# Inverting the diagonal blocks of two groups of heads with the same instructions, in one long kernel

## The chip, the cores and the metric

The kernel runs on one core of a Trainium2 chip. Its metric is the device time of one execution in microseconds (us), the median of several. Engines are named as in the profile: PE (matrix products; PEld its weight loads), DVE (vector), ACT (activations), POOL (general), and SP, whose queue issues most DMAs.

## The reference

The program computes several transformer layers on 256 context and 256 latent tokens, with a width of 1024: an RWKV-7/Mamba mixer, a feed-forward, neighbourhood attention, a mixture of experts, and two further blocks. What is changed lies in the first mixer, in RWKV's recurrence, which runs over eight heads of 64 and in both directions:

```python
def _rwkv7_scan(s0, r, w, k, v, a, b):
    def step(S, inp):
        r_t, w_t, k_t, v_t, a_t, b_t = inp
        sa = jnp.einsum('bhvk,bhk->bhv', S, a_t)
        S = S * w_t[:, :, None, :] + sa[..., None] * b_t[:, :, None, :] + v_t[..., None] * k_t[:, :, None, :]
        return S, jnp.einsum('bhvk,bhk->bhv', S, r_t)
    ...
    s_fin, ys = lax.scan(step, s0, xs)
```

Beside it the program computes adaLN's shifts and scales, products of a small conditioning vector with large weights (`w_ada`, `ada_w_2`), which have nothing to do with the recurrence but are needed after it.

## The kernel before, in words

The scan is done by chunks of 64 tokens. Inside a chunk the tokens act on each other through a triangular matrix, which is inverted: a 64x64 matrix is split in two diagonal blocks of 32x32, each is inverted by forward substitution, and the corner is made with small matmuls.

The work is cut into eight groups k = (th, sh, u): th is context or latent tokens, sh the half of the chunks, u the half of the heads. Each group has 32 diagonal blocks. Its stages are:

- **P(k)**: decays, keys and scores (matmuls `lw`, `ic`, `ci`, `sc`; DVE masks the scores into EA in line 966 and into S in line 968), then `rw_blocks`. That writes the diagonal blocks from EA to DRAM (`dsc`) and reads them back as E, one block to four partitions, with each of the four read all of `dsc`; it also makes a zero matrix X with ones on the diagonal (POOL) and the transposed corner (`et`). At its end `rw_update` makes the `bt` transposes.
- **I(k)**: 31 steps of forward substitution on DVE, a product (line 1012) and a sum (line 1013) each. A partition handles 8 of a block's 32 columns, so step i works on i//4+1 columns.
- **Q(k)**: the inverse X goes through DRAM (`dx`, line 1018) back into EA (line 1022), on SP's and ACT's DMA queues; three sets of 16 small matmuls `m` and copies (lines 1036, 1038 and 1045) make the corner.
- **C(k)**: two chain steps (`rw_step`). A step makes Z from UV with EA and from the state YM with AR, copies it to zs (line 1072), makes the second half of Z from zs with EA, copies it to UV (line 1081), makes the new Z from UV with S and YM with AR, and adds (line 1095, into YM).
- **F**: normalises and gates the output.

ORDER names the order in which the stages are written out. A scheduler then sets each engine's queue. It is a fixed list: an engine that waits for one instruction starts none behind it. Matmuls of adaLN (line 377, called `ada`, with the row's transposes `adat` in line 386) get the lowest priority there and so stand where the model of the scheduler has PE free. Their weights come as tiles `raw` of 512 KB through SP's queue (line 353) into five buffers.

Of the kernel before, what the change touches and what calls it, by code (L numbers as in the profile page):

```python
# [8 lines left out]
F32 = mybir.dt.float32  # L9
# [3 lines left out]
ALU = mybir.AluOpType  # L13
# [4 lines left out]
D = 1024  # L18
# [29 lines left out]


F1, F2, F3, F4, F5, F6, F7 = 2, 2, 2, 2, 2, 2, 1  # L50
ORDER = 'P0 I0 P1 I1 Q0 C0 P2 I2 Q1 C1 P3 I3 Q2 C2 F0 P4 I4 Q3 C3 F1 P5 I5 Q4 C4 P6 I6 Q5 C5 P7 I7 Q6 C6 F2 Q7 C7 F3'
HOT = 0
WB = 1, 1
HOTM = 100000
# [1 line left out]
NROW = 5  # L56
NU, ND, NM, NYM, NB, NR, NW, NMB = 8, 3, 4, 6, 2, 6, 4, 7
NFIRST = 3000
XENG = '0'
QE = 's'  # L60
NADA = 12

# [3 lines left out]
class Builder:  # L66
# [474 lines left out]
    def mixer_consts(s):  # L541
        nc, I, mx = s.nc, s.I, s.mx
        s.lora = mx.tile([128, 3, 512], F32, name="lora")
        nc.scalar.dma_start(s.lora, I["lora"])
        c = s.cmix = mx.tile([128, 896], F32, name="cmix")
        nc.scalar.dma_start(c, I["c_mix"])
        s.tri = c[:, 0:256].rearrange("p (d t) -> p d t", d=2)
        s.maskr = c[:, 256:768].rearrange("p (d h e t) -> p d h e t", d=2, h=2, e=2)
        s.bd = c[:, 768:896]
        s.c0 = mx.tile([128, 14], F32, name="c0")  # L550
        nc.vector.tensor_tensor(s.c0, s.pcols("mu0"), s.pcols("mu1"), op=ALU.add)
        nc.vector.tensor_scalar(s.c0, s.c0, -1.0, 1.0, op0=ALU.mult, op1=ALU.add)

        s.kah = mx.tile([128, 4], F32, name="kah")
        nc.vector.tensor_scalar(s.kah, s.pcols("ka"), 0.5, None, op0=ALU.mult)
        s.ka1 = mx.tile([128, 4], F32, name="ka1")
        nc.vector.tensor_scalar(s.ka1, s.kah, -1.0, 1.0, op0=ALU.mult, op1=ALU.add)
        s.kkh = mx.tile([128, 4], F32, name="kkh")
        nc.vector.tensor_scalar(s.kkh, s.pcols("kk"), -1.0, None, op0=ALU.mult)

        s.PT = mx.tile([128, 4, 2, 2, 2, 2, 2], F32, name="PT")
        s.la = mx.tile([128, 4, 2, 8], F32, name="la")
        nc.vector.memset(s.PT, 0.0)
        s.par = mx.tile([128, 4], F32, name="par")
        nc.scalar.dma_start(s.par, I["c_x0"])
        s.misc = [mx.tile([128, 512], F32, name="misc%d" % i) for i in range(3)]
        s.iv = [mx.tile([128, 136], F32, name="iv%d" % i) for i in range(2)]
        s.zs = [mx.tile([128, 256], F32, name="zs%d" % i) for i in range(2)]
# [187 lines left out]
    def rw_blocks(s, th, sh, u):  # L756


        a, v = s.nc.scalar, s.nc.vector
        E = s.E[th, sh, u] = s.unit(nm="E").rearrange("p (s t) -> p s t", s=32)  # L760
        EA = s.EA[th, sh, u].rearrange("p d j c h t -> p (d j c) h t")
        D = s.dr.tile([4, 8, 32, 32], F32, name=s.n("dsc"))
        for i in (0, 2, 1, 3):
            r = slice(32 * i, 32 * i + 32)
            s.dq(i < 2).dma_start(D[i].rearrange("q s t -> s q t"), EA[r, :, 1 - i // 2, 32 * (i % 2):32 * (i % 2) + 32])
        D = D.rearrange("i q s t -> (i q) s t")
        for r in range(4):
            s.dq(r % 2).dma_start(E[r::4], D)
        X = s.row(nm="X")
        s.xt[th, sh, u] = X  # L770
        s.nc.gpsimd.memset(X[:, 0:256], 0.0)
        for r in range(4):
            s.nc.gpsimd.tensor_copy(X[:, r:256:36], s.par[:, r:r + 1].to_broadcast([128, 8]))
        xt = X[:, 256:512].rearrange("p (q t) -> p q t", q=8)
        p = s.ps("et")[:, 0:256].rearrange("p (q t) -> p q t", q=8)
        for q in range(8):
            for h in range(2):
                o = 64 - 64 * h
                s.mm(p[o + 32:o + 64, q], lhsT=EA[o:o + 32, q, h, 32:64], rhs=s.ident[o:o + 32, o:o + 32], start=True, stop=True, tile_position=(o, o + 32))
        for h in range(2):  # L780
            o = 96 - 64 * h
            (v.tensor_copy if h else a.copy)(xt[o:o + 32], p[o:o + 32])
# [14 lines left out]

    def rwkv(s):
        x = [(k // 4, k // 2 % 2, k % 2) for k in range(8)]
        X = {}  # L800

        def P(k):
            s.rw_tiles(*x[k])
            yield from s.rw_prep(*x[k])
            s.rw_blocks(*x[k])
            yield
            s.rw_update(*x[k])
            yield

        def I(k):  # L810
            X[k] = s.rw_inverse(*x[k])
            for i in range(31):
                next(X[k])
                if i % 8 == 7:
                    yield

        def Q(k):
            yield from X.pop(k)

        def C(k):  # L820
            if k % 4 < 2:
                s.rw_values(x[k][0], x[k][2])
            yield from s.rw_chain(*x[k])

        def F(k):
            yield from s.rw_finish(k // 2, k % 2)
        for o in ORDER.split():
            s.dump("@%s" % o)
            yield from {"P": P, "I": I, "Q": Q, "C": C, "F": F}[o[0]](int(o[1]))
# [153 lines left out]
    def rw_values(s, th, u):  # L983
# [12 lines left out]
        for h in range(2):  # L996
            s.nc.scalar.copy(UV[HS[h], :, :, h].rearrange("p j c t -> p (j c) t"), q8(p[HS[h]]))

    def rw_inverse(s, th, sh, u):

        nc = s.nc
        v, a = nc.vector, nc.scalar
        mm = s.mm
        E = s.E.pop((th, sh, u))

        Xt = s.xt.pop((th, sh, u))
        X = Xt[:, 0:256].rearrange("p (m t) -> p m t", m=8)
        e = nc.gpsimd if XENG[(4 * th + 2 * sh + u) % len(XENG)] == "1" else nc.vector
        for i in range(31):
            m, n = i // 4 + 1, 31 - i  # L1010
            t = s.iv[i % 2][:, :m * n].rearrange("p (m n) -> p m n", m=m)
            e.tensor_tensor(t, X[:, 0:m, i:i + 1].to_broadcast([128, m, n]), E[:, i:i + 1, i + 1:].to_broadcast([128, m, n]), op=ALU.mult)
            e.tensor_tensor(X[:, 0:m, i + 1:], X[:, 0:m, i + 1:], t, op=ALU.add)
            yield
        Dx = s.dr.tile([32, 32, 32], F32, name=s.n("dx"))
        dst = Dx.rearrange("q (m r) t -> r q m t", r=4)
        for r in range(4):
            s.dq(r % 2).dma_start(dst[r], X[r::4])
        EA = s.EA[th, sh, u].rearrange("p d j c h t -> p (d j c) h t")
        for i in (0, 2, 1, 3):  # L1020
            r = slice(32 * i, 32 * i + 32)
            s.dq(i < 2).dma_start(EA[r, :, 1 - i // 2, 32 * (i % 2):32 * (i % 2) + 32], Dx[8 * i:8 * i + 8].rearrange("q s t -> s q t"))
        xt = Xt[:, 256:512].rearrange("p (q t) -> p q t", q=8)

        R = [(slice(64 - 64 * h, 96 - 64 * h), slice(96 - 64 * h, 128 - 64 * h), 64 - 64 * h) for h in range(2)]
        p1, p2 = [s.ps("m1")[:, 0:256].rearrange("p (q t) -> p q t", q=8) for _ in range(2)]
        for q in range(8):
            for h in range(2):
                r1, r2, o = R[h]
                mm(p1[r1, q], lhsT=EA[r1, q, h, 0:32], rhs=s.ident[r1, r1], start=True, stop=True, tile_position=(o, o))  # L1030
        for q in range(8):
            for h in range(2):
                r1, r2, o = R[h]
                mm(p2[r1, q], lhsT=xt[r2, q], rhs=EA[r2, q, h, 32:64], start=True, stop=True, tile_position=(o + 32, o))
        for h in range(2):
            (v.tensor_copy if h else a.copy)(xt[R[h][0]], p1[R[h][0]])
        for h in range(2):
            (v.tensor_copy if h else a.copy)(EA[R[h][0], :, h, 32:64], p2[R[h][0]])
        yield
        for q in range(8):  # L1040
            for h in range(2):
                r1, r2, o = R[h]
                mm(p1[r1, q], lhsT=xt[r1, q], rhs=EA[r1, q, h, 32:64], start=True, stop=True, tile_position=(o, o))
        for h in range(2):
            (v.tensor_copy if h else a.copy)(EA[R[h][0], :, h, 32:64], p1[R[h][0]])
        yield

    def rw_step(s, th, sh, u, i, new):
# [1198 lines left out]
def host_arrays(inp):  # L2247

    A = {k: np.asarray(v) for k, v in inp.items()}
    f = np.float32  # L2250
    out = {}
# [46 lines left out]
    q = 63 - np.arange(128) % 64  # L2298
# [3 lines left out]
    i = np.arange(128)  # L2302
# [5 lines left out]
    j = np.arange(128) % 64  # L2308
# [12 lines left out]
    c = 2 * np.pi * ((i[:, None] * i[None, :]) % 128) / 128  # L2321
    n = 2 * np.pi * ((tt[:, None] * tt[None, :]) % 256) / 256
# [3 lines left out]
    i = np.arange(128)  # L2326
    k, t = i[:, None], i[None, :]
# [4 lines left out]
    for h in range(2):  # L2332
# [2 lines left out]
    seg = [k > t, k <= t, k < t, k >= t]  # L2335
    out["c_mix"] = np.concatenate([np.where(m, f(-0.5 * E05), f(0)) for m in tri] + [m.astype(f) for m in mask]
                                  + [same.astype(f)], axis=1).astype(f)
    out["c_x0"] = np.tile(np.eye(4, dtype=f), (32, 1))
    out["c_seg"] = np.concatenate([m.astype(f) for m in seg], axis=1)
    return out  # L2340

# [13 lines left out]
```

## Time and profile before

| | us |
|---|---|
| median of three executions | 2830.1 (2818.82 to 2833.47) |
| the profiled execution | 2819.89, span 2818.1 |
| PE busy in the span | 2632.0 (93%) |
| PEld | 2093.3 (74%) |
| DVE | 1885.5 (67%) |
| ACT | 1289.0 (46%) |
| POOL | 170.9 (6%) |

A share is of the whole span, over stages with different limits. The recurrence is the stretch from about 255 to 668 us, so the rows below are of that stretch. The granted clock is PE's, as a share of 2.4 GHz.

### The profile page before, as it was taken

The page shows a single profiled execution, that of the slowest core. Times are in us where ns is not written, and L with a number is a line of the kernel's source. Part 1 is how long each engine was busy: PE and PEld are TensorE (multiplying, and loading weights), DVE is VectorE, ACT ScalarE, POOL GpSimd, SP SyncE. Part 2 cuts the span into 40 slices and gives each one's busy share as a digit, 9 for nine tenths or more (in the row PEclk, how much of TensorE's full clock was granted, in tenths as well). Part 3 has the DMA queues.
Part 4 walks back from the last instruction along what each step waited for, and adds up shares of the span by engine and source line. Part 5 has one row for each costly group of instructions (what it writes and reads, how often), then busy time and mean ns, then how long its engine had stood idle before and what let it go on. Part 6 is the DMA issues. An engine that isn't in the chain of part 4 may idle for free. (4 is left out here: it accounts for less than half of the span.)

```text
span 2818.1 us, 40635 instructions
## 1 busy us (share of the span) xinstructions
PE 2632.0 (93%) x15434; PEld 2093.3 (74%) x15434; DVE 1885.5 (67%) x3039; ACT 1289.0 (46%) x1760; POOL 170.9 (6%) x276
## 2 busy tenths in 40 slices
PE   6999899997999998999999999999998987997798
PEld 3876456654888887887788888888876866996797
DVE  4657877744434457445798988998896566555655
ACT  3532122112332223444688777777775443443343
POOL 0112223210000000000000000000000000000000
PEclk8999888988999998999899999999998998998899
DMA  6324876668323233433599999999997324663562
GB/s 237 89 73 162 271 243 199 217 229 296 101 90 103 92 90 90 105 90 109 188 373 347 347 343 345 363 359 345 357 342 252 122 90 149 186 189 100 160 184 75
DMA packets 324444, 570.83 MB, mean 203 GB/s; under 512 B 61752, under 2 KB 167608, under 8 KB 324240
## 3 DMA queue, kind: packets, MB, share of 16 engines
q1 hardware_dynamic: 304064, 544.61, 57.2%
q10 hardware_dynamic: 16784, 11.74, 1.4%
q0 software_dynamic: 3392, 11.80, 1.3%
q8 instruction: 123, 2.02, 0.3%
q14 instruction: 81, 0.66, 0.1%
HBM read 563.79 MB, written 4.28 MB: 202 GB/s over the span
## 5 line engine op out<-in xcount | busy, mean ns | idle before, releaser
L204 DVE TENSOR_TENSOR wl<-raw,wh 128x1024 fp32r<-128x1024 f32 x828 | 984.6, 1221 | 427.6 <-ACT wh L203 414.0
L203 ACT CAST wh<-raw 128x1024 fp32r<-128x1024 f32 x828 | 839.0, 1051 | 511.4 <-issue 191.4
L249 PE MATMUL ws<-xL,wh 128*128 128x256 f32 (+1 forms) x1392 | 456.5, 328 | 3.6 <-DVE xL L204 3.6
L248 PE MATMUL ws<-xH,wh 128*128 128x256 f32 (+1 forms) x1392 | 458.5, 332 | 0.9 <-DVE xTf L482 0.7
L250 PE MATMUL ws<-xH,wl 128*128 128x256 f32 (+1 forms) x1392 | 457.6, 329 | 0.5 <-DVE wl L204 0.5
L248 PEld LDWEIGHTS ws<-xH,wh 128*128 128x128 f32 x1392 | 265.8, 192 | 35.7 <-issue 10.1
L249 PE MATMUL mw<-wl,eH 128*128 128x512 f32 (+1 forms) x768 | 289.7, 377 | 1.4 <-DVE wl L204 1.2
L250 PEld LDWEIGHTS ws<-xH,wl 128*128 128x128 f32 x1392 | 265.8, 191 | 30.7 <-issue 6.8
L248 PE MATMUL mw<-wh,eH 128*128 128x512 f32 (+1 forms) x768 | 286.2, 375 | 1.8 <-ACT wh L203 1.8
L249 PEld LDWEIGHTS ws<-xL,wh 128*128 128x128 f32 x1392 | 265.8, 191 | 29.2 <-DVE xL L204 4.6
L250 PE MATMUL mw<-wh,eL 128*128 128x512 f32 (+1 forms) x768 | 286.4, 373 | 0.0
L377 PE MATMUL ada<-raw,act 128*32 128x512 f32 x768 | 175.6, 728 | 32.2 <-DMA raw<-in_w_ada 13.1
L249 PEld LDWEIGHTS mw<-wl,eH 128*128 128x128 f32 x768 | 145.1, 189 | 33.3 <-DVE wl L204 8.8
L248 PEld LDWEIGHTS mw<-wh,eH 128*128 128x128 f32 x768 | 145.0, 189 | 28.3 <-ACT wh L203 3.1
L250 PEld LDWEIGHTS mw<-wh,eL 128*128 128x128 f32 x768 | 145.0, 189 | 24.1
L249 PE MATMUL y<-wl,uH 128*128 128x512 f32 x352 | 139.6, 397 | 2.0 <-DVE wl L204 2.0
L250 PE MATMUL y<-wh,uL 128*128 128x512 f32 x352 | 135.7, 391 | 0.0
L248 PE MATMUL y<-wh,uH 128*128 128x512 f32 x352 | 115.0, 390 | 0.0
L471 PE MATMUL xT<-ident,xn 128*128 128x128 f32 x160 | 34.9, 394 | 82.1 <-DVE xn L449 51.5
L377 PEld LDWEIGHTS ada<-raw,act 128*32 128x32 f32 x768 | 28.4, 122 | 105.5 <-issue 36.1
L248 PE MATMUL o<-wh,mH 128*128 128x512 f32 x256 | 100.0, 390 | 0.0
L249 PE MATMUL o<-wl,mH 128*128 128x512 f32 x256 | 99.9, 390 | 0.0
(483 smaller groups left out, 4070.2 us busy)
## 6 DMA issues: line engine op xcount, KB each, us to landing
raw<-in_moe_w SPq DMA_DIRECT2D x528, 512.0 KB
raw<-in_mlp_w SPq DMA_DIRECT2D x128, 512.0 KB
raw<-in_w_ada SPq DMA_DIRECT2D x96, 512.0 KB
raw<-in_ada_w SPq DMA_DIRECT2D x96, 512.0 KB
raw<-in_ffn_w SPq DMA_DIRECT2D x66, 512.0 KB
raw<-in_mix_w_in SPq DMA_DIRECT2D x24, 512.0 KB
raw<-in_na_w_qkv SPq DMA_DIRECT2D x24, 512.0 KB
raw<-in_w_in SPq DMA_DIRECT2D x24, 512.0 KB
```

The source lines that it names most:

```text
L203: s.nc.scalar.copy(H, raw)
L204: s.nc.vector.tensor_tensor(L, raw, H, op=ALU.subtract)
L248: mm(out, lhsT=lH, rhs=rH, start=start, stop=False)
L249: mm(out, lhsT=lH, rhs=rL, start=False, stop=False)
L250: mm(out, lhsT=lL, rhs=rH, start=False, stop=stop)
L377: nc.tensor.matmul(ps[32 * j:32 * j + 32, :], lhsT=act[:, k, :], rhs=x[j // 2][:, j % 2 * 512:j % 2 * 512 + 512], start=(k == 0), stop=(k ...
L471: nc.tensor.transpose(p[:, j, t * 128:t * 128 + 128], xn[t][:, k * 128:k * 128 + 128], s.ident)
```

## The change

E and X become a matter of a pair of groups (the same th and sh, both u). A block now has two partitions for four, a partition 16 of its columns; the two groups of a pair fill the 128 partitions together. `rw_solve` runs the 31 steps once for the pair, on i//2+1 columns in step i, and at its end puts the DMAs of X to `dx` and back into EA for both groups. `rw_inverse` is left with the small matmuls. The zeros and ones of X are made at the start of `rw_solve`. `XENG`, a choice of engine that was always DVE, goes. ORDER is written by pairs.

```diff
@@ -48,7 +48,8 @@
 F1, F2, F3, F4, F5, F6, F7 = 2, 2, 2, 2, 2, 2, 1
-ORDER = 'P0 I0 P1 I1 Q0 C0 P2 I2 Q1 C1 P3 I3 Q2 C2 F0 P4 I4 Q3 C3 F1 P5 I5 Q4 C4 P6 I6 Q5 C5 P7 I7 Q6 C6 F2 Q7 C7 F3'
+
+ORDER = 'P0 P1 I0 P2 Q0 Q1 C0 P3 C1 I2 P4 Q2 Q3 C2 P5 C3 F0 F1 I4 P6 Q4 Q5 C4 P7 C5 I6 Q6 Q7 C6 C7 F2 F3'
 HOT = 0
 WB = 1, 1
 HOTM = 100000
@@ -56,7 +57,6 @@
 NROW = 5
 NU, ND, NM, NYM, NB, NR, NW, NMB = 8, 3, 4, 6, 2, 6, 4, 7
 NFIRST = 3000
-XENG = '0'
 QE = 's'
 NADA = 12
@@ -561,7 +561,7 @@
         s.PT = mx.tile([128, 4, 2, 2, 2, 2, 2], F32, name="PT")
         s.la = mx.tile([128, 4, 2, 8], F32, name="la")
         nc.vector.memset(s.PT, 0.0)
-        s.par = mx.tile([128, 4], F32, name="par")
+        s.par = mx.tile([128, 2], F32, name="par")
         nc.scalar.dma_start(s.par, I["c_x0"])
         s.misc = [mx.tile([128, 512], F32, name="misc%d" % i) for i in range(3)]
         s.iv = [mx.tile([128, 136], F32, name="iv%d" % i) for i in range(2)]
@@ -757,21 +757,19 @@
         a, v = s.nc.scalar, s.nc.vector
-        E = s.E[th, sh, u] = s.unit(nm="E").rearrange("p (s t) -> p s t", s=32)
+        if u == 0:
+            s.E[th, sh] = s.unit(nm="E").rearrange("p (s t) -> p s t", s=32)
+            s.xt[th, sh] = s.row(nm="X")
+        E = s.E[th, sh]
         EA = s.EA[th, sh, u].rearrange("p d j c h t -> p (d j c) h t")
         D = s.dr.tile([4, 8, 32, 32], F32, name=s.n("dsc"))
         for i in (0, 2, 1, 3):
             r = slice(32 * i, 32 * i + 32)
             s.dq(i < 2).dma_start(D[i].rearrange("q s t -> s q t"), EA[r, :, 1 - i // 2, 32 * (i % 2):32 * (i % 2) + 32])
         D = D.rearrange("i q s t -> (i q) s t")
-        for r in range(4):
-            s.dq(r % 2).dma_start(E[r::4], D)
-        X = s.row(nm="X")
-        s.xt[th, sh, u] = X
-        s.nc.gpsimd.memset(X[:, 0:256], 0.0)
-        for r in range(4):
-            s.nc.gpsimd.tensor_copy(X[:, r:256:36], s.par[:, r:r + 1].to_broadcast([128, 8]))
-        xt = X[:, 256:512].rearrange("p (q t) -> p q t", q=8)
+        for r in range(2):
+            s.dq(r).dma_start(E[2 * u + r::4], D)
+        xt = s.xt[th, sh][:, 256 * u:256 * u + 256].rearrange("p (q t) -> p q t", q=8)
         p = s.ps("et")[:, 0:256].rearrange("p (q t) -> p q t", q=8)
         for q in range(8):
             for h in range(2):
@@ -797,7 +795,6 @@
     def rwkv(s):
         x = [(k // 4, k // 2 % 2, k % 2) for k in range(8)]
-        X = {}
         def P(k):
             s.rw_tiles(*x[k])
@@ -808,14 +805,10 @@
             yield
         def I(k):
-            X[k] = s.rw_inverse(*x[k])
-            for i in range(31):
-                next(X[k])
-                if i % 8 == 7:
-                    yield
+            yield from s.rw_solve(*x[k][:2])
         def Q(k):
-            yield from X.pop(k)
+            yield from s.rw_inverse(*x[k])
         def C(k):
             if k % 4 < 2:
@@ -996,31 +989,42 @@
         for h in range(2):
             s.nc.scalar.copy(UV[HS[h], :, :, h].rearrange("p j c t -> p (j c) t"), q8(p[HS[h]]))
+    def rw_solve(s, th, sh):
+
+        nc = s.nc
+        v = nc.vector
+        E = s.E.pop((th, sh))
+
+        Xr = s.row(nm="X")
+        nc.gpsimd.memset(Xr, 0.0)
+        for r in range(2):
+            nc.gpsimd.tensor_copy(Xr[:, r:512:34], s.par[:, r:r + 1].to_broadcast([128, 16]))
+        X = Xr.rearrange("p (m t) -> p m t", m=16)
+        for i in range(31):
+            m, n = i // 2 + 1, 31 - i
+            t = s.iv[i % 2][:, :m * n].rearrange("p (m n) -> p m n", m=m)
+            v.tensor_tensor(t, X[:, 0:m, i:i + 1].to_broadcast([128, m, n]), E[:, i:i + 1, i + 1:].to_broadcast([128, m, n]), op=ALU.mult)
+            v.tensor_tensor(X[:, 0:m, i + 1:], X[:, 0:m, i + 1:], t, op=ALU.add)
+            if i % 8 == 7:
+                yield
+        for u in range(2):
+            Dx = s.dr.tile([32, 32, 32], F32, name=s.n("dx"))
+            dst = Dx.rearrange("q (m r) t -> r q m t", r=2)
+            for r in range(2):
+                s.dq(r).dma_start(dst[r], X[2 * u + r::4])
+            EA = s.EA[th, sh, u].rearrange("p d j c h t -> p (d j c) h t")
+            for i in (0, 2, 1, 3):
+                r = slice(32 * i, 32 * i + 32)
+                s.dq(i < 2).dma_start(EA[r, :, 1 - i // 2, 32 * (i % 2):32 * (i % 2) + 32], Dx[8 * i:8 * i + 8].rearrange("q s t -> s q t"))
+        yield
+
     def rw_inverse(s, th, sh, u):
         nc = s.nc
         v, a = nc.vector, nc.scalar
         mm = s.mm
-        E = s.E.pop((th, sh, u))
-
-        Xt = s.xt.pop((th, sh, u))
-        X = Xt[:, 0:256].rearrange("p (m t) -> p m t", m=8)
-        e = nc.gpsimd if XENG[(4 * th + 2 * sh + u) % len(XENG)] == "1" else nc.vector
-        for i in range(31):
-            m, n = i // 4 + 1, 31 - i
-            t = s.iv[i % 2][:, :m * n].rearrange("p (m n) -> p m n", m=m)
-            e.tensor_tensor(t, X[:, 0:m, i:i + 1].to_broadcast([128, m, n]), E[:, i:i + 1, i + 1:].to_broadcast([128, m, n]), op=ALU.mult)
-            e.tensor_tensor(X[:, 0:m, i + 1:], X[:, 0:m, i + 1:], t, op=ALU.add)
-            yield
-        Dx = s.dr.tile([32, 32, 32], F32, name=s.n("dx"))
-        dst = Dx.rearrange("q (m r) t -> r q m t", r=4)
-        for r in range(4):
-            s.dq(r % 2).dma_start(dst[r], X[r::4])
         EA = s.EA[th, sh, u].rearrange("p d j c h t -> p (d j c) h t")
-        for i in (0, 2, 1, 3):
-            r = slice(32 * i, 32 * i + 32)
-            s.dq(i < 2).dma_start(EA[r, :, 1 - i // 2, 32 * (i % 2):32 * (i % 2) + 32], Dx[8 * i:8 * i + 8].rearrange("q s t -> s q t"))
-        xt = Xt[:, 256:512].rearrange("p (q t) -> p q t", q=8)
+        xt = s.xt[th, sh][:, 256 * u:256 * u + 256].rearrange("p (q t) -> p q t", q=8)
         R = [(slice(64 - 64 * h, 96 - 64 * h), slice(96 - 64 * h, 128 - 64 * h), 64 - 64 * h) for h in range(2)]
         p1, p2 = [s.ps("m1")[:, 0:256].rearrange("p (q t) -> p q t", q=8) for _ in range(2)]
@@ -1043,6 +1047,8 @@
                 mm(p1[r1, q], lhsT=xt[r1, q], rhs=EA[r1, q, h, 32:64], start=True, stop=True, tile_position=(o, o))
         for h in range(2):
             (v.tensor_copy if h else a.copy)(EA[R[h][0], :, h, 32:64], p1[R[h][0]])
+        if u:
+            del s.xt[th, sh]
         yield
     def rw_step(s, th, sh, u, i, new):
@@ -2335,7 +2341,7 @@
     seg = [k > t, k <= t, k < t, k >= t]
     out["c_mix"] = np.concatenate([np.where(m, f(-0.5 * E05), f(0)) for m in tri] + [m.astype(f) for m in mask]
                                   + [same.astype(f)], axis=1).astype(f)
-    out["c_x0"] = np.tile(np.eye(4, dtype=f), (32, 1))
+    out["c_x0"] = np.tile(np.eye(2, dtype=f), (64, 1))
     out["c_seg"] = np.concatenate([m.astype(f) for m in seg], axis=1)
     return out
```

The first place is on PE, where the first `m` of the second pair stands (EA_3322 before and EA_3093 now are the same group, context tokens, second half of the chunks, first half of the heads). Before:

```order
1006 L377 MATMUL ada_2221<-raw_2248,act_87 32x512 x2
1007 L377 MATMUL ada_2221<-raw_2249,act_87 32x512 x2
1008 L377 MATMUL ada_2221<-raw_2256,act_87 32x512 x2
1009 L274 MATMUL m_3896<-ident,EA_3322 32x32 x16
1010 L274 MATMUL m_3897<-EA_3322,X_3420 32x32 x16
1011 L377 MATMUL ada_2221<-raw_2257,act_87 32x512 x2
1012 L377 MATMUL ada_2221<-raw_2264,act_87 32x512 x2
1013 L377 MATMUL ada_2221<-raw_2265,act_87 32x512 x2
1014 L274 MATMUL sc_4155<-AR_4130,bk_4137 128x128 x4
```

And now:

```order
974 L274 MATMUL Z_3985<-YM_3388,AR_3122 64x64 x2
975 L274 MATMUL Z_3985<-UV_3334,EA_3093 64x64 x2
976 L274 MATMUL lw_3750<-lora,misc_302 128x256
977 L274 MATMUL Z_3620<-zs_307,EA_2892 64x64 x8
978 L274 MATMUL lw_3750<-lora,misc_303 128x256
979 L377 MATMUL ada_2221<-raw_2230,act_87 32x512
980 L274 MATMUL m_3872<-ident,EA_3093 32x32 x2
981 L274 MATMUL ic_3751<-misc_302,lora 128x128 x2
982 L274 MATMUL ic_3751<-misc_303,lora 128x128 x2
983 L274 MATMUL m_3872<-ident,EA_3093 32x32 x4
984 L274 MATMUL Z_3649<-UV_3565,S_2944 128x64
985 L274 MATMUL Z_3649<-YM_3586,AR_2921 64x64
```

Before, three ada tiles stand directly ahead of the group's `m`; now matmuls of the chain and of the group after next do, with one half of an ada tile.

The second place is on PE again, at the last inversion: EA_5267 was the last group of all, and EA_4483 and EA_4844 are now the last two. Before:

```order
1387 L274 MATMUL Z_5581<-UV_3218,EA_4884 64x64 x2
1388 L274 MATMUL Z_5581<-YM_5530,AR_4913 64x64 x2
1389 L274 MATMUL Z_5581<-UV_3218,EA_4884 64x64 x2
1390 L386 MATMUL adat_2608<-ident,adar_2538 128x128 x4
1391 L274 MATMUL m_5688<-ident,EA_5267 32x32 x12
1392 L274 MATMUL Z_5581<-zs_306,EA_4884 64x64 x8
1393 L274 MATMUL m_5688<-ident,EA_5267 32x32 x4
1394 L274 MATMUL m_5689<-EA_5267,X_5365 32x32 x16
1395 L377 MATMUL ada_2619<-raw_2591,act_90 32x512 x2
1396 L377 MATMUL ada_2619<-raw_2592,act_90 32x512 x2
```

And now:

```order
1378 L377 MATMUL ada_2540<-raw_2558,act_90 32x512 x2
1379 L377 MATMUL ada_2540<-raw_2567,act_90 32x512 x2
1380 L377 MATMUL ada_2540<-raw_2568,act_90 32x512 x2
1381 L377 MATMUL ada_2540<-raw_2575,act_90 32x512 x2
1382 L377 MATMUL ada_2540<-raw_2576,act_90 32x512 x2
1383 L377 MATMUL ada_2540<-raw_2583,act_90 32x512 x2
1384 L377 MATMUL ada_2540<-raw_2584,act_90 32x512 x2
1385 L386 MATMUL adat_2608<-ident,adar_2538 128x128 x4
1386 L274 MATMUL m_5171<-ident,EA_4483 32x32 x16
1387 L274 MATMUL m_5172<-EA_4483,X_4572 32x32 x16
1388 L377 MATMUL ada_2619<-raw_2591,act_90 32x512 x2
1389 L377 MATMUL ada_2619<-raw_2592,act_90 32x512 x2
```

The `m` of the last inversion stood behind Z matmuls with the row transposes `adat`; now that of the pair stands behind seven ada tiles of these rows and `adat`, and the other group's `m` and Z follow after it.

The third place is on DVE, where the last solve ends. Before:

```order
1051 L1012 TENSOR_TENSOR iv_305<-X_5365,E_5355 128x16
1052 L1013 TENSOR_TENSOR X_5365<-X_5365,iv_305 128x8x2
1053 L1012 TENSOR_TENSOR iv_304<-X_5365,E_5355 128x8
1054 L1013 TENSOR_TENSOR X_5365<-X_5365,iv_304 128x8
1055 L1095 TENSOR_TENSOR YM_5530<-Z_5560,YM_5530 128x512
1056 L380 TENSOR_TENSOR adar_2538<-ada_2540,adar_2538 128x512
1057 L1072 COPY zs_306<-Z_5581 128x256
1058 L391 COPY mcol_98<-adat_2608 128x4x2 x4
1059 L1081 COPY UV_3218<-Z_5581 64x2x2x64
1060 L1036 COPY X_5365<-m_5688 32x256
1061 L1038 COPY EA_5267<-m_5689 32x8x32
```

And now:

```order
796 L1006 TENSOR_TENSOR iv_305<-X_5091,E_4571 128x30
797 L1007 TENSOR_TENSOR X_5091<-X_5091,iv_305 128x15x2
798 L1006 TENSOR_TENSOR iv_304<-X_5091,E_4571 128x16
799 L1007 TENSOR_TENSOR X_5091<-X_5091,iv_304 128x16
800 L380 TENSOR_TENSOR adar_2538<-ada_2540,adar_2538 128x512
801 L391 COPY mcol_98<-adat_2608 128x4x2 x4
802 L1040 COPY X_4572<-m_5171 32x256
803 L1042 COPY EA_4483<-m_5172 32x8x32
804 L1049 COPY EA_4483<-m_5171 32x8x32
805 L1040 COPY X_4572<-m_5227 32x256
806 L1042 COPY EA_4844<-m_5228 32x8x32
```

The last steps have twice as many columns (16 for 8) in as many instructions, and the copies of two groups follow for those of one. DVE has 496 instructions of the solve before and 248 now.

## Rows read from the trace of the kernel before

**Rows 1.** Busy time by stretch: length, engines, clock, DMA share, GB/s; stage and its end.

```profile
255.00:668.00 413.00, 383.61 (x3693) 219.21 (x3693) 280.43 (x913) 77.57 (x161) 94.65 (x162) 0.87 0.71 234
...
600.00:668.00 68.00, 59.36 (x450) 26.76 (x445) 23.66 (x56) 8.89 (x16) 6.32 (x9) 0.80 0.69 232
```

**Rows 2.** What PE waited for, 255 to 668: total us, times, longest.

```profile
PE ada L377 <- DMA raw<-in_ada_w: 10.4, 17, 3.0
PE ada L377 <- DMA raw<-in_w_ada: 7.6, 8, 2.0
PE adat L386 <- DVE adar L380: 2.9, 3, 1.2
...
PE sc L274 <- DVE iv L1012: 1.4, 2, 0.9
PE et L274 <- DVE EA L966: 1.2, 1, 1.2
PE Z L274 <- DVE EA L1045: 1.2, 1, 1.2
PE m L274 <- DMA EA<-dx: 0.9, 1, 0.9
PE sc L274 <- DVE bk L913: 0.6, 1, 0.6
```

**Rows 3.** PE groups, 255 to 668: busy us, mean ns, idle before, releasers.

```profile
L377 PE MATMUL ada<-raw,act 128*32 128x512 f32 x671 | 151.1, 727 | 19.9 <-DMA raw<-in_ada_w 10.4 <-DMA raw<-in_w_ada 7.6 <-issue 1.5
L274 PE MATMUL Z<-UV,S 128*128 128x64 f32 x256 | 55.4, 308 | 0.0
L274 PE MATMUL Z<-YM,AR 64*64 64x64 f32 x448 | 54.9, 248 | 0.0
...
L274 PE MATMUL Z<-UV,EA 64*64 64x64 f32 x256 | 17.4, 232 | 0.0
L274 PE MATMUL Z<-zs,EA 64*64 64x64 f32 x256 | 14.0, 238 | 1.2 <-DVE EA L1045 1.2
...
L278 PE MATMUL bt<-ident,bk 128*128 128x128 f32 x64 | 11.7, 319 | 0.7 <-POOL bk L976 0.5 <-DVE X L782 0.2
```

**Rows 4.** DVE groups, 255 to 640, columns as above.

```profile
L1013 DVE TENSOR_TENSOR X<-X,iv 128x60 f32<-128x60 f32 (+24 forms) x248 | 63.6, 256 | 5.9
L1012 DVE TENSOR_TENSOR iv<-X,E 128x60 f32<-128x60 f32 (+24 forms) x248 | 60.0, 242 | 16.7 <-DMA E<-dsc 10.9
...
L1095 DVE TENSOR_TENSOR YM<-Z,YM 128x512 f32<-128x512 f32 x14 | 9.7, 690 | 37.9 <-PE Z L274 37.9
```

**Rows 5.** DVE, shapes apart, in the last solve.

```profile
L1012 DVE TENSOR_TENSOR iv<-X,E 128x60 f32<-128x60 f32 x3 | 0.7, 222 | 0.1
```

**Rows 6.** Timeline of the last inversion: start us, us, instruction, idle before.

```profile
562.30 0.42 DVE L966 TENSOR_TENSOR EA<-sc,cmix 128x256 f32<-128x256 f32 x1 [3.90 <-PE sc L274]
...
571.93 0.19 DVE L1012 TENSOR_TENSOR iv<-X,E 128x31 f32<-128x31 f32 x1 [4.03 <-DMA E<-dsc]
...
589.60 0.17 DVE L1013 TENSOR_TENSOR X<-X,iv 128x8 f32<-128x8 f32 x1
...
599.13 0.57 PE L274 MATMUL m<-ident,EA 32*32 32x32 f32 x24 [0.95 <-DMA EA<-dx]
```

**Rows 7.** Stretch at a lower clock, and two PE rows of the timeline about its start.

```profile
508.00:517.50 9.50, 9.50 (x94) 7.23 (x97) 6.73 (x20) 1.17 (x3) 4.36 (x4) 0.50 0.14 34
...
506.80 0.43 PE L274 MATMUL Z<-UV,S 128*128 128x64 f32 x2
...
508.22 0.69 PE L274 MATMUL Z<-UV,S 128*128 128x64 f32 x2
```

**Rows 8.** Timeline of PE: the row with which the stage ends.

```profile
667.80 0.66 PE L386 MATMUL adat<-ident,adar 128*128 128x128 f32 x4 [0.85 <-DVE adar L380]
```

## The prediction

> **What bounds the kernel now.** I read the table by stretch first, then what TensorE waited for, then the groups of PE and DVE, then single instructions. The change touches only the recurrence, which fills 255 to 668 us of the span [rows 1]. There PE is busy 383.61 of 413 us, DVE 280.43, ACT and POOL under 100 each; the granted clock averages 0.87 and the DMA engines are 0.71 busy [rows 1]. PE's queue is a fixed order of the recurrence's small matmuls with the adaLN matmuls (L377) put between them. All that PE waits for in these 413 us is in one list [rows 2]: 18.0 us for adaLN's own weights (10.4 and 7.6), 2.9 for the adaLN row sum on DVE, and for what the change touches 1.4 (scores behind a solve's instruction), 1.2 and 1.2 (two EA results late on DVE), 0.9 (m behind EA<-dx) and 0.6 (bk): 5.3 us together. The other way round, DVE's chain sum YM waits 37.9 us for PE [rows 4]. So the stage is a full PE queue, and the solve is almost wholly beside it.
>
> **What the change removes.** The solve is 248 products and 248 sums on DVE, 60.0 and 63.6 us, 123.6 together [rows 4]. An undisturbed one takes 222 ns with 60 elements and 166 with 8 [rows 5], so 1.08 ns an element on a fixed 157. One solve works on 1560 elements in 31 steps in each of the two operations (the sum over i of (i//4+1)(31-i)): 62 x 0.157 + 2 x 1560 x 0.00108 = 13.1 us, and eight are 105 us. That 123.6 is more is other work at the same time. The pair's solve has the same 62 instructions with (i//2+1)(31-i), 2856 elements: 9.7 + 6.2 = 15.9 us, and four are 64 us. So 41 us of DVE's busy time go, or 48 if the surplus shrinks in proportion (123.6 x 64/105 = 75). What of it lies on the path is at most what PE waited for behind it, the 5.3 us above; of these the m wait and the masks behind scores will have successors. I take 4 off.
>
> **What it moves, and the waits that this makes.** No matmul goes or comes: m, et, Z and the scores are the same, so PE's work is the same to within the order. The order changes. Both groups of a pair now need the scores of the second before the solve may begin, and all their m matmuls wait for one solve. From the last score's mask to m there is one chain, read at the last group of before: the mask starts at 562.30, the first product at 571.93 (so 9.6 us through dsc and E), the last sum ends at 589.77, m starts at 599.13 (9.4 us through dx and EA) [rows 6]. The pair's solve is 15.9 us, some 1.9 of gaps (62 x 0.03: the last group's 62 instructions took 17.8 us, with other DVE work among them), and about 3 us of the chain's own copies and sums that stand between, 21 in all. The chain is then 9.6 + 21 + 9.4 = 40 us.
>
> What stands in PE's queue in that time decides. For the second pair, between the last score of group 3 and the first m of group 2, the new order has 24 Z<-UV,S, 32 Z<-YM,AR, 24 Z<-UV,EA, 24 Z<-zs,EA, 15 ada and 8 bt matmuls, each two rows in the trace. At the means of [rows 3], busy time by count, this is 48 x 0.216 + 64 x 0.123 + 48 x 0.068 + 48 x 0.055 + 30 x 0.225 + 16 x 0.183 = 10.4 + 7.9 + 3.3 + 2.6 + 6.8 + 2.9 = 33.9 us, and some 4 for the adat, et, m and lw among them: 38 at the stage's mean clock. At full clock it would be about a tenth less (the clock term below), 34. So PE stands still for 2 to 6 us at the first m of that pair; I take 4. In before the same m comes behind three ada tiles, and the one wait for EA<-dx in the stage is the 0.9 us of the last group [rows 2, 6]. For the first pair PE has the in_w_ada matmuls in plenty, and m comes at about the time of before: 0. For the last pair the new order puts nine ada tiles, each 1.05 us as four rows at full clock, ahead of m, where before had Z matmuls; that covers most of it. For pairs 3 and 4 together I take 3. Both ends: nothing (cover holds everywhere), and 27 us if three pairs each lose 9, the length of the EA path that has no cover of its own.
>
> **Edits at no cost.** E is loaded with two DMAs a group for four: half of 8 x 512 KB, 2 MB of the roughly 97 MB that 234 GB/s [rows 1] makes of 413 us. The queue's tail runs by weights (the last ada's row sum ends the stage at 667.80 [rows 8]) and five weight buffers let no load run further ahead, so bytes saved at 300 us are not had at 660: between -9 (2.1 MB at 234 GB/s) and 0, taken 0. The two dx stores of a pair and the EA loads behind them sit in SP's queue among weight loads; a weight load stuck behind the dx wait costs PE what the five buffers don't hold. The trace shows no such loss of its own beside the 18.0 us; bounds 0 and +4, taken 0. X is cleared by POOL just ahead of the solve, not with the scores; it has the E transfer (most of 9.6 us) to lie under: 0, and 2 us a pair, 8 in all, if it starts only after E is in. The m copies stay as they were.
>
> **The clock.** In 508.00 to 517.50 PE was busy without a gap at a granted 0.50, so 1.2 GHz, and a pair of Z<-UV,S rows took 0.69 us after 0.43 just before at 2.4 GHz [rows 7]; the fall came amid a full run of Z matmuls. A mean of 0.87 over 413 us says that about 2 x 0.13 x 413 = 107 us went at 1.2 GHz; at 0.43/0.69 of the time they would be 67, so the half clock costs 40 us. The last stretch, with many ada matmuls, had 0.80 [rows 1], so more ada does not by itself bring the clock. The new order crowds small matmuls in some places and ada in others. Nothing in the rows says to which side that falls: 20 us of these 40 either way, taken 0.
>
> The Trainium skill, "TensorE: Matmul & The Clock Gate", section "HAM oscillation", has waits for data as what throws the clock back; the rows above show it fall with no gap in front. By the page's rule the new wait at the second pair would bring its own loss; that price is in the slower rival.
>
> **Sum.** -4 + 4 + 3 = +3 us on the profiled execution's own 2819.9 (span 2818.1): about 2823. That execution is 10 us below the median of the runs shown, 2830.1, and the same step on the median gives 2833, no change that can be told: a measurement of this kernel separates 0.5%, 14 us, from none.
>
> **Rivals.** *DVE sets PE's pace.* If PE's records hide waits, a shorter solve gets the chain's copies and sums out earlier everywhere: the 5.3 us go, the 2.9 for the adaLN sum too, and PE crosses more of the stage at full clock, of which I allow half the 40 us. Minus 8 and minus 20, less the 4 at the second pair: 24 off, 2806 on the median. For it: one DVE instruction in two of the stage goes. Against: YM and the masks wait for PE, not PE for them. [...] The list of what PE waited for, 5.3 us behind the solve, speaks against [rows 2].
>
> *The pair's solve becomes PE's wait.* Scores of the second group, E, solve, dx, EA lie end to end with all of the pair's m behind, and PE has too little else in the order at pairs 2, 3 and 4. With 9 us at each, 27, less the 4: +23 to 2853. It decides from where PE's waits for EA<-dx or for the m copies pass some 18 us in sum; half clock behind each wait would add to it. For it: the count of matmuls above falls short of 40 us even at the mean clock. Against: ada in front of the last pair's m.
>
> *The order alone.* The same waits, but the clock lies worse by 20 of the half-clock's 40 us and nothing else: 2850; I count its chance with the one before, and the mirror of it with the first.
>
> **Chances.** Forecast 0.45; DVE's pace (with a better clock) 0.23; the pair's wait or a worse clock 0.32. Faster by over 0.5% 0.23, within 0.45, slower 0.32. The range takes in most of both sides: 2808 to 2858; the forecast's own is 2820 to 2844.
>
> **What would show it.** DVE's solve at 64 to 75 us in 248 rows and DVE down some 45 us in the stage; PE's busy time within 10 us of 384; the first m of the second pair with a wait of 2 to 6 us for EA<-dx; the last adat 0 to 8 us later, reckoned from 255. I am wrong if PE's waits for EA<-dx sum to over 18 us, if PE's waits vanish and the stage is 15 us shorter at the same clock, or if the mean clock in the stage moves by more than 0.05.

## The result, and the profile after

The changed kernel takes 2864.2 us (2860.6 to 2871.7, four runs), the one before 2827.3 us over the same sessions: a ratio of 1.0133, interval 1.0103 to 1.0164, so 37 us slower. The forecast was 2833 and no change that can be told, with a range up to 2858.

All of it lies in the recurrence. From its end to the end of the span both profiled executions take the same: the first matmul of the stage behind it (`xs`) starts at 719.26 of a span of 2861.1, so 2141.8 us are left; before it was 676.48 of 2818.1, 2141.6 left. The stage's last `adat`, 667.80 before [rows 8], is now at 711.10, 43.3 us later. PE's timeline after, with start, length and what ended the wait:

```profile
711.10 0.66 PE L386 MATMUL adat<-ident,adar 128*128 128x128 f32 x4 [0.79 <-DVE adar L380]
719.26 2.07 PE L248 MATMUL xs<-wh,oH 128*128 128x512 f32 x4 [7.50 <-ACT wh L203]
```

The busy times of the stage after, in the columns of [rows 1] (length; PE, PEld, DVE, ACT, POOL busy; clock, DMA share, GB/s), to 712 us:

```profile
255.00:712.00 457.00, 412.14 (x3730) 237.76 (x3726) 238.90 (x667) 78.32 (x164) 97.33 (x150) 0.82 0.62 209
```

DVE has 42 us less to do (280.43 before [rows 1]), PE is busy 28 us longer (383.61 before) with the same matmuls, at a mean clock of 0.82 for 0.87. The DVE groups, to be held against [rows 4], show where the 42 went, and that the chain's sum YM now waits 51.2 us for PE where it waited 37.9:

```profile
L1007 DVE TENSOR_TENSOR X<-X,iv 128x126 f32<-128x126 f32 (+22 forms) x124 | 38.2, 308 | 3.4
L1006 DVE TENSOR_TENSOR iv<-X,E 128x126 f32<-128x126 f32 (+22 forms) x124 | 37.1, 299 | 13.6 <-DMA E<-dsc 8.5 <-DMA raw<-in_ada_w 2.0
...
L1101 DVE TENSOR_TENSOR YM<-Z,YM 128x512 f32<-128x512 f32 x14 | 9.7, 691 | 51.2 <-PE Z L274 51.2
```

What PE waited for, as in [rows 2]: total, times, longest.

```profile
PE ada L377 <- DMA raw<-in_ada_w: 18.8, 22, 2.6
PE ada L377 <- DMA raw<-in_w_ada: 9.9, 11, 2.8
...
PE Z L274 <- DVE UV L1087: 3.7, 2, 3.3
PE bo L274 <- POOL bon L938: 2.7, 2, 2.0
PE ada L377 <- issue: 1.8, 2, 1.3
PE adat L386 <- DVE adar L380: 1.6, 2, 0.8
PE m L274 <- ACT EA L1042: 1.4, 1, 1.4
...
PE m L274 <- DMA EA<-dx: 0.8, 1, 0.8
```

The wait that the forecast looked for, m behind EA<-dx, is 0.8 us. The weights' waits grew from 18.0 to 28.7.

The chain shows what the order by pairs does. Its sixteen state writes YM stood 13 to 36 us apart before, from 347 to 635 us. Now the first is at 386, and between the eighth and the ninth there are 84 us, in which the first pair of the latent tokens is prepared:

```profile
500.69 0.69 DVE L1101 TENSOR_TENSOR YM<-Z,YM 128x512 f32<-128x512 f32 x1 [2.16 <-PE Z L274]
...
585.06 0.68 DVE L1101 TENSOR_TENSOR YM<-Z,YM 128x512 f32<-128x512 f32 x1
```

And by stretch: in 365 to 389, where the first pair's m, the scores and the first chain steps stand next to each other, PE is busy to the last tenth and at 1.2 GHz; the stretch of the last eight chain sums runs at a mean of 0.79.

```profile
365.00:389.00 24.00, 23.90 (x259) 17.97 (x257) 8.98 (x22) 2.99 (x8) 3.40 (x3) 0.50 0.37 120
...
585.00:690.00 105.00, 97.88 (x922) 56.09 (x914) 38.42 (x113) 11.26 (x28) 15.24 (x18) 0.79 0.57 195
```

### The profile page after: what moved, and what is told of

It reads as the page before. It is cut to its first block, busy times and chain, and to the rows that moved or that the text cites. A ratio compares the mean times of both kernels' runs of the same rounds, so it can differ in the third digit from the quotient of the medians.

```text
span 2861.1 us, 40305 instructions
## 1 busy us (share of the span) xinstructions
PE 2658.2 (93%) x15434; PEld 2110.0 (74%) x15434; DVE 1844.2 (64%) x2791; ACT 1289.0 (45%) x1760; POOL 168.5 (6%) x248
```

## An account of the stage

To compare many kernels I split the stage, from 255 us to the start of `xs`, in the profiled execution of each. Every PE record, up to the start of the next, is valued at the mean that its group has at 2.4 GHz in the stage of before: the sum is the work. What the records took beyond it is the clock's loss (a few us of it are records stretched at full clock); the gaps between records are idle. The last column is what PE's records took at a granted 0.50. All in us, with the median of the runs beside them (before stood at 2825 to 2828 from session to session):

| kernel | median | stage | work | clock | idle | PE records at 1.2 GHz |
|---|---|---|---|---|---|---|
| before | 2826 | 421 | 348 | 36 | 37 | 109 |
| after | 2864 | 464 | 349 | 63 | 52 | 155 |
| e1, joint, near the old order | 2857 | 462 | 348 | 64 | 50 | 180 |
| e2, single, order by pairs | 2891 | 495 | 351 | 83 | 61 | 203 |
| e3, after, DMAs on ACT | 2872 | 479 | 350 | 69 | 60 | 166 |
| e4, before, DMAs on ACT | 2887 | 483 | 348 | 74 | 60 | 172 |
| e5, after, even ada | 2853 | 453 | 350 | 56 | 46 | 143 |
| e6, before, even ada | 2868 | 472 | 350 | 70 | 53 | 161 |
| e7, single, order of e1 | 2901 | 497 | 348 | 85 | 63 | 200 |
| e8, e1, even ada | 2874 | 474 | 348 | 65 | 61 | 156 |
| e9, single, X's buffer earlier | 2875 | 478 | 351 | 65 | 63 | 166 |
| e10, joint but the first pair | 2875 | 489 | 351 | 80 | 58 | 203 |
| e11, e9 with the last pair joint | 2879 | 486 | 354 | 77 | 55 | 196 |
| e12, single, I4 moved behind P5 | 2836 | 436 | 350 | 42 | 45 | 114 |
| e13, joint, other order | 2847 | 447 | 347 | 52 | 49 | 153 |
| e14, joint, other order | 2854 | 454 | 348 | 62 | 45 | 174 |
| e15, joint, other order | 2878 | 477 | 350 | 68 | 59 | 180 |
| e16, joint, sparse order | 2918 | 527 | 350 | 105 | 72 | 257 |

The work is 347 to 354 us in all eighteen. Some of PE's records are missing from a trace, and what they took stands under idle, so work and idle are good to some 7 us. Of the 43 us by which the profiled stage grew, 27 are PE at the lower clock or stretched, and 15 are idle; PE's waits for ada's weights grew by 10.7. The rest of the program moves by no more than 5 us.

Clock and idle are not two separate losses. The low stretch around 365 to 389 began at 358.5, amid ada matmuls that waited for their weights: from 352 on PE was busy for 3.36 of 6.5 us, and the last row below spans the fall (four ada rows take 1.05 us at full clock).

```profile
352.00:358.50 6.50, 3.36 (x14) 0.58 (x16) 0.49 (x2) 0.60 (x1) 1.44 (x10) 1.00 0.69 197
...
357.05 1.05 PE L377 MATMUL ada<-raw,act 128*32 128x512 f32 x4 [2.34 <-DMA raw<-in_w_ada]
358.29 1.78 PE L377 MATMUL ada<-raw,act 128*32 128x512 f32 x4 [0.20 <-DMA raw<-in_w_ada]
```

I counted the falls of the granted clock in the two stages by what PE did in the 5 us ahead of each; the 5 us are a choice of mine, and 3 us give the same. In the stage of before the clock falls 18 times: 12 times after PE was busy for over 95% of them, with 68 us at 0.50 behind these falls, and 6 times after PE had stood idle for more, with 46 us. In the changed kernel it is 10 times with 72 us, and 10 times with 94 us (idle time at 0.50 included). So the added time at the lower clock lies almost wholly behind falls that came after PE had waited. What else kept the clock down once it fell, this count does not tell.

## The experiments

Each ratio is to the kernel before in the same sessions. The theories are named in the expectations. The first four runs ask for the order, the joint solve, and the DMA queue.

**e1** (joint solve, stages as nearly as before as the pairs allow):

```diff
-ORDER = 'P0 P1 I0 P2 Q0 Q1 C0 P3 C1 I2 P4 Q2 Q3 C2 P5 C3 F0 F1 I4 P6 Q4 Q5 C4 P7 C5 I6 Q6 Q7 C6 C7 F2 F3'
+ORDER = 'P0 P1 I0 Q0 C0 P2 Q1 C1 P3 I2 Q2 C2 F0 P4 Q3 C3 F1 P5 I4 Q4 C4 P6 Q5 C5 P7 I6 Q6 C6 F2 Q7 C7 F3'
```

> The changed kernel with the stages written out nearly as before: 'P0 P1 I0 Q0 C0 P2 Q1 C1 P3 I2 Q2 C2 F0 P4 Q3 C3 F1 P5 I4 Q4 C4 P6 Q5 C5 P7 I6 Q6 C6 F2 Q7 C7 F3'. Theory 1 (the order by pairs costs it: chain steps pause and ada matmuls come in clumps): most of the 37 us come back, 2820 to 2840. Theory 2 (the joint solve itself costs it, since both groups wait for the second's scores and m for one long solve): still 2855 to 2875.

Measured 2857 us, 1.0115 (1.0082 to 1.0149). Seven of the 37 came back at most: theory 1 as stated falls, and theory 2 stands for the moment.

**e2** (the kernel before in the order by pairs):

```diff
-ORDER = 'P0 I0 P1 I1 Q0 C0 P2 I2 Q1 C1 P3 I3 Q2 C2 F0 P4 I4 Q3 C3 F1 P5 I5 Q4 C4 P6 I6 Q5 C5 P7 I7 Q6 C6 F2 Q7 C7 F3'
+ORDER = 'P0 P1 I0 I1 P2 Q0 Q1 C0 P3 C1 I2 I3 P4 Q2 Q3 C2 P5 C3 F0 F1 I4 I5 P6 Q4 Q5 C4 P7 C5 I6 I7 Q6 Q7 C6 C7 F2 F3'
```

> The kernel before, each group solved by itself, with the stages in the order of the changed kernel (I0 I1 where it has I0, and so on). Theory 1: slow without any joint solve, 2850 to 2875. Theory 2: near before, 2820 to 2840, as each group's solve may start with its own scores.

Measured 2891 us, 1.0238 (1.0198 to 1.0279). Theory 2 falls: without any joint solve this order costs 66 us. It is also slower than the 2850 to 2875 that theory 1 gave. Under the same order of stages the joint solve is 27 us faster, not slower. The stage of e2:

```profile
255.00:750.00 495.00, 433.81 (x3737) 252.29 (x3736) 278.62 (x919) 81.28 (x166) 101.93 (x166) 0.78 0.60 201
```

**e3 and e4** (the DMAs of the inversion on ACT's queue, in the changed kernel and in the one before):

```diff
-QE = 's'
+QE = 'a'
```

> The changed kernel with all DMAs of the inversion (dsc, E, dx, EA) on ACT's queue, so that SP's queue holds the weight loads alone. Theory 3 (SP stands before a pair's dx and EA loads, and the weights behind them come late: PE waits 28.7 us for weights after, 18.0 before): 10 to 25 us of the 37 come back, 2840 to 2854, and the waits for raw fall under 18 us. Theories 1 and 2: 2855 to 2875.

> The kernel before with the same DMAs on ACT's queue, the control of the run before. Theory 3 as a matter of pairs alone: within 8 us of before. If the queue costs both kernels, 10 us or more faster than before.

Measured 2872 us, 1.0165 (1.0124 to 1.0205), and 2887, 1.0226 (1.0189 to 1.0262). Theory 3 falls: with the inversion's DMAs off SP's queue the weights' waits of e3 are still 26.6 us,

```profile
PE ada L377 <- DMA raw<-in_ada_w: 17.5, 26, 2.8
PE ada L377 <- DMA raw<-in_w_ada: 9.1, 11, 1.9
```

and e4 was not the quiet control that was expected: it is 62 us slower. The scheduler laid PE's queue out anew in e4 as well, so the 62 us are not shown to be the price of the DMA queue. That was the first hint that nearly any edit costs this stage tens of us.

Next came the place of the ada matmuls (theory C) against the pair's waits (theory P).

**e5, e6 and e8** (ada's steps written among the recurrence's, for after, before and e1):

```diff
-        with s.tc.high_priority(offset=APRI):
-            s.filler(999)
-        s.run(s.rwkv())
+        s.work = 0
+        s.weave((s.rwkv(), 1), fill=1.16)
+        s.filler(999)
```

> The changed kernel with adaLN's steps written between the recurrence's, one after each equal part of its matmul work, for all of them at the lowest priority. Theory C (the order leaves stretches with few ada matmuls; there PE runs at 1.2 GHz): time at 1.2 GHz in the stage falls from 155 us to 125 or less and the run to 2825 to 2850. Theory P (the joint solve and the waits behind it): 2855 to 2880, the clock as it was.

> The kernel before with adaLN's steps written between the recurrence's in the same way: the control. Theory C: 2810 to 2835, as its ada matmuls stand rather evenly already; and the gap to the run before this one shrinks to under 15 us. Theory P: a gap of some 35 us stays.

> e1 with adaLN's steps between the recurrence's as in e5. Theory C: 2820 to 2850, time at 1.2 GHz under 130 us for 178 in e1. Theory P: as e1, 2850 to 2865.

Measured 2853 us, 1.0112 (1.0084 to 1.0140); 2868, 1.0176 (1.0127 to 1.0225); and 2874, 1.0194 (1.0163 to 1.0224). The joint kernel gains 11 us, which falls between the ranges of theories C and P, with 143 us at 1.2 GHz where it had 155 and theory C said 125 or less; the single one loses 41, and e8 loses 17 on e1, beyond both theories. So an even spread by itself is not what the kernel before had: in e6 the last ada round ends at 684 us and the stage at 727, so the end stands without any. Theory C fails in its form, theory P too, since the gap between joint and single turned round.

**e7** (single, in the stage order of e1):

```diff
-ORDER = 'P0 I0 P1 I1 Q0 C0 P2 I2 Q1 C1 P3 I3 ...'
+ORDER = 'P0 P1 I0 I1 Q0 C0 P2 Q1 C1 P3 I2 I3 ...'
```

> The kernel before, each group solved by itself, with the stages written in the order of e1 (I0 I1 where that has I0, and so on). In its queue some stretches of 15 us of work have no ada matmul at all. Theory C: as slow as e2, 2870 to 2900, time at 1.2 GHz over 170 us. Theory P: faster than e1, under 2845, since no group waits for its partner's solve.

Measured 2901 us, 1.0286 (1.0261 to 1.0311): 44 us slower than its joint twin e1, with 200 us at 1.2 GHz. Theory C said 2870 to 2900 and over 170; theory P, under 2845, fails.

Then whether a late first chain is the cause (theory L) or simply another layout of PE's queue (theory R).

**e9** (single; the work and the order of stages of before, X's buffer taken ahead of the DMAs of `dsc` and E; one more small constant is loaded; the run's code is the changed kernel's with no pair joint, and the edit is written here as one of before; dots stand for what is left out):

```diff
         E = s.E[th, sh, u] = s.unit(nm="E")...
+        X = s.row(nm="X")
         ...
         for r in range(4):
             s.dq(r % 2).dma_start(E[r::4], D)
-        X = s.row(nm="X")
```

> Every group solved by itself, in the order of stages of before, and the same work; only X's buffer is taken a few lines earlier (ahead of E's DMAs), by which the scheduler lays PE's queue out otherwise from the middle of the stage on. Theory R (before's queue is a lucky one, and any other costs tens of us): 2845 to 2890, with time at 1.2 GHz over 140 us. Theory L (the cost is that a pair's first chain starts late, behind P1): within 10 us of before.

Measured 2875 us, 1.0169 (1.0127 to 1.0211). This is the run that settles most: the same work, the same stages, and 50 us are lost, more than the change under study loses. Theory L does not account for it: the first YM stands at 348 us, as in before (347). The scheduler sets the queues of all engines, so the run shows what a new layout can cost, not which queue it is. Its stage, with as much work on DVE as before:

```profile
255.00:733.00 478.00, 415.37 (x3737) 236.22 (x3736) 284.69 (x919) 80.60 (x166) 100.36 (x166) 0.81 0.62 208
```

**e10, e11 and e12** (joint but for the first two groups; only the last pair joint, else as e9; single with one stage moved):

```diff
+JOINT = ((0, 1), (1, 0), (1, 1))     # e10: P0 I0 P1 I1 Q0 C0 P2 Q1 C1 P3 I2 ...
+JOINT = ((1, 1),)                    # e11: as before up to ... P6 Q5 C5 P7 I6 Q6 C6 F2 Q7 C7 F3
-... F0 P4 I4 Q3 C3 F1 P5 I5 ...      # e12
+... F0 P4 Q3 C3 F1 P5 I4 I5 ...
```

> The first two groups are solved singly at the start as in before, the other three pairs jointly. Theory L: most of the 37 us come back, 2815 to 2840. Theory R: 2845 to 2890, like e9.

> Only the last pair is solved jointly, the six groups before it singly in the order of before; its queue is that of e9 up to there. Against e9 it tells the joint solve alone: if that relieves the stage, 10 to 25 us under e9; if waits for the partner cost, over it by as much. Theory L: within 10 us of before.

> The kernel before with one change of order at the second half's start: P4 Q3 C3 F1 P5 I4 I5 where it had P4 I4 Q3 C3 F1 P5 I5; singly solved. Theory L (a late chain costs its delay): 10 to 30 us slower. Theory R: 20 to 60 us slower, with PE's full-clock work the same and time at 1.2 GHz over 140 us.

Measured 2875 us, 1.0160 (1.0110 to 1.0211); 2879, 1.0176 (1.0127 to 1.0226); 2836, 1.0037 (1.0010 to 1.0064). e10 falls where theory R put it. e11 is 3 us over e9, within what the two medians scatter: one joint solve in place of two single ones neither gains nor loses there. e12 loses 11 us, less than the 20 to 60 of theory R, with 114 us at 1.2 GHz where R said over 140; here the 10 to 30 of theory L were met, after L had failed in e9, e10 and e11.

Last, four kernels with the changed one's code and only ORDER altered, picked by their PE queue. A fit to the fourteen kernels above said what to expect: the time grows with the stretches of the queue that have few ada matmuls.

> Joint solve, stages 'P0 P1 I0 Q0 C0 P2 Q1 P3 C1 I2 Q2 C2 F0 Q3 P4 P5 C3 F1 I4 Q4 C4 P6 Q5 C5 P7 I6 Q6 C6 F2 Q7 C7 F3'. The 14 kernels so far follow 2838 us + 11.2 us for each us by which the ada share of the 15 us of work about a point of PE's queue falls short of 15%, less 0.63 us per us of ada behind the last other matmul (it explains 0.86 of their variance). For this queue: 2844. Theory R (layout of the queue): 2825 to 2855. Theory P (the joint solve's waits): 2855 to 2875.

> Joint solve, 'P0 P1 I0 P2 Q0 C0 Q1 C1 P3 I2 P4 Q2 C2 P5 Q3 C3 F0 I4 F1 Q4 Q5 P6 P7 C4 I6 C5 Q6 C6 Q7 C7 F2 F3'. By the same sum 2843. Theory R: 2825 to 2855; theory P: 2855 to 2875.

> Joint solve, 'P0 P1 I0 Q0 C0 Q1 P2 P3 C1 I2 Q2 C2 Q3 F0 P4 C3 F1 P5 I4 Q4 Q5 P6 C4 P7 C5 I6 Q6 C6 F2 Q7 C7 F3'. By the same sum 2844. Theory R: 2825 to 2855; theory P: 2855 to 2875.

> Joint solve, 'P0 P1 P2 I0 Q0 Q1 C0 P3 P4 C1 I2 Q2 Q3 C2 C3 P5 F0 P6 F1 I4 Q4 Q5 C4 C5 P7 I6 Q6 Q7 C6 C7 F2 F3': its ada matmuls are used up early, and some 75 us of the queue's end have none. By the same sum 2951. Theory R: 2900 to 2960, with time at 1.2 GHz over 200 us and PE's full-clock work still 348 to 354. Theory P: 2855 to 2885.

Measured 2847 us, 1.0062 (1.0043 to 1.0082); 2854, 1.0098 (1.0069 to 1.0128); 2878, 1.0184 (1.0158 to 1.0211); 2918, 1.0315 (1.0287 to 1.0342). The sum said 2844, 2843, 2844 and 2951. The first was met, the second missed by 11 us and the third by 34, and the fourth by 33 on the other side. Theory R's ranges held for e13, e14 and e16, the last with 257 us at 1.2 GHz and 350 of work; e15 lies beyond both theories. So the layout decides between 2847 and 2918 for one and the same joint work. The fit picks out the slow e16, but gave 2843 to 2844 to three orders that lie 32 us apart, so the share of ada matmuls in the queue is not the whole of it. The end of e16, where its queue has no ada matmul at all, with all engines in one row:

```profile
690.00:780.00 90.00, 78.80 (x734) 63.40 (x733) 27.99 (x67) 15.37 (x32) 11.47 (x14) 0.50 0.07 13
```

PE was busy for 78.80 of these 90 us, and the whole stretch passed at 1.2 GHz. Here the clock fell, at 685, after a nearly full run of Z matmuls without ada:

```profile
680.00:685.00 5.00, 4.79 (x46) 3.94 (x44) 4.69 (x14) 0.47 (x2) 1.43 (x2) 0.84 0.00 0
```

## Why the prediction was wrong

Right, or nearly: DVE's solve takes 75.3 us where 64 to 75 were given, and DVE loses 42 us in the stage where "some 45" was said. A product with 136 elements takes 301 ns and one with 16 180, so 1.01 ns an element on a fixed 164; the forecast's line, 1.08 on 157, gave 304 and 174.

```profile
L1006 DVE TENSOR_TENSOR iv<-X,E 128x136 f32<-128x136 f32 x4 | 1.2, 301 | 0.1
...
L1006 DVE TENSOR_TENSOR iv<-X,E 128x16 f32<-128x16 f32 x4 | 0.7, 180 | 0.1
```

PE's work stayed the same. The wait at the second pair came at the place named, with 0.76 us for the 2 to 6:

```profile
417.80 0.25 PE L274 MATMUL m<-ident,EA 32*32 32x32 f32 x4 [0.76 <-DMA EA<-dx]
```

The step that failed is the costing of the order: "No matmul goes or comes ... so PE's work is the same to within the order. The order changes." I priced that by the waits that could be seen at one instruction, 4 and 3 us, put the clock at "20 us of these 40 either way, taken 0", and the weights' waits at "bounds 0 and +4, taken 0". In the runs the new queue is itself the largest term. The order by pairs alone cost 66 us (e2), and of its profiled stage's growth of 74 us the lower clock took 47, idle time 24 and the work 3; in the changed kernel the first two are 27 and 15, and the weights' waits grew by 10.7, above my bound of 4. The clock was read from one fall with no gap ahead of it [rows 7]; in the changed kernel half of the falls came after PE had waited, and it is behind these that time at 0.50 grew, from 46 to 94 us. "Nothing in the rows says to which side that falls" was wrong in one respect: the kernel before stood at one end. Of seventeen other layouts none has less time at 1.2 GHz and none less idle time, even where nothing was changed but a buffer's turn (e9). Among the layouts tried here, a rearranged queue lost every time.

The forecast failed without meeting any of the three conditions it named for being wrong: the waits for EA<-dx stayed at 0.8 us, the stage was not shorter, and the mean clock moved by no more than 0.05. PE's busy time did leave the 10 us about 384 that it was given (412).

The rival that came nearest in time, 2853 for "the pair's solve becomes PE's wait", is not what happened: PE's waits for EA<-dx are 0.8 us in sum, not over 18. "The order alone" had the right place and too small a price. (Its 2850 leaves out the forecast's own 3 us of waits; with the same waits, as it says, it is 2853.) "DVE sets PE's pace" has something for it once the queue is spoilt: under like orders of stages the joint solve was faster by 27 (e2 to after), 44 (e7 to e1) and 15 us (e6 to e5), and from e9 to e11 one joint solve did nothing. Since PE's queue differs inside each of these pairs too, how much of this is the joint solve's own stays open; no pair shows it to cost anything beyond 3 us.

Also open: why the kernel before's layout is so good. That the clock stays low through stretches with few ada matmuls is seen in e16's last 90 us, which have none, and in 365 to 389 of the changed kernel (12 ada rows there, 3.85 us), though in the second it had fallen amid ada matmuls. That few ada matmuls are what keeps it low is not shown: a queue held fixed with only the ada matmuls taken out was not tried, since the scheduler lays the queue out anew for each edit. Nor was a joint order found that is as fast as the kernel before; the best, e13, is 0.6% slower.

## What to carry to other kernels

When a scheduler sets a queue, an edit's cost has two parts, its instructions and the new layout, and in a stage with a full PE the second can be the larger; price it by a control that relays the queue and changes no work, before crediting or blaming the edit. Split a stage into work at full clock, time lost at the lower clock, and idle: here the first was 347 to 354 us in every kernel, so all that any order could win or lose was in the other two. And a wait that was searched for at one instruction and not found says nothing of the clock.

## What the runs showed of the hardware

The granted clock fell to 0.50 both after PE had waited (3.36 of 6.5 us busy ahead of 358.5 in the changed kernel) and after a nearly full run (4.79 of 5 us ahead of 685 in e16). It stayed there while PE was busy for 23.90 of 24 us in 365 to 389, and for 78.80 of 90 at the end of e16. PE's records at 1.2 GHz took from 153 (e13) to 257 us (e16) of the stage with the same matmuls, in kernels that differ in ORDER alone. And one DVE product of the solve took 180 ns with 16 elements a partition and 301 with 136.
